# The placing of adaLN steps, three weight splits and two gate low parts in a fused attention–retention layer

## The chip, the cores and the metric

The kernel runs on one core of a Trainium2 chip as one launch. The metric is the device time of that launch in microseconds; a verdict compares medians of several runs on the same chip. One more execution was taken with the hardware profiler, and all rows shown are of that one. The engines are PE (TensorE, matrix products), DVE (VectorE), ACT (ScalarE), POOL (GpSimd) and SP (SyncE, which here issues the DMAs). Each engine works through its own list of instructions strictly in order; semaphores hold an instruction until what it needs has been written.

## The reference

The layer takes 1024 tokens of width 1024, in float32. What matters here:

```python
mod = silu(c) @ w_ada + b_ada                  # adaLN: shift1, scale1, gate1, shift2, scale2, gate2
h = rmsnorm(x, norm1_w) * (1 + scale1) + shift1
proj = h @ w_in                                # qa ka va | iq ik iw | qr kr vr gr | ga gb
qa, ka, iq, ik = partial_rope(...)             # rotation of the first 16 of 64 channels of a head
# per block of 128 tokens: index scores choose 256 keys for each token
s_h   = einsum('bqhd,bsd->bqhs', iq, ik) * idx_scale
score = einsum('bqh,bqhs->bqs', iw * w_scale, relu(s_h))
idx   = top_k(score, 256)
att   = sparse attention of qa over the chosen keys of ka, va
ret   = chunkwise retention of rotated qr, kr with vr
x = x + gate1 * ((sigmoid(ga) * (att @ w_attn_proj)
                  + sigmoid(gb) * (groupnorm(ret) * silu(gr) @ w_ret_proj)) @ w_out)
x = x + gate2 * swiglu_ffn(rmsnorm(x) * (1 + scale2) + shift2);  out = rmsnorm(x)
```

## The kernel before

Every large product is made of float32 numbers split in two parts: ACT copies a weight tile to a rounded high part (`whi`), POOL or DVE subtracts to get the low part (`wlo`), and PE forms hi·hi, hi·lo and lo·hi. `split_weight` (L77 the ACT copy, L80 the POOL subtraction) does it for tiles of 128x512, `split_block` (L958, L959) for the later streams.

A recording layer lists every instruction with a priority and writes out one fixed order per engine; `turns_after(ins, other)` only demands that `ins` stands behind `other` in the order of its engine. So an edit in one place can move instructions on several engines.

**Stage one: V and index scores.** The loop over the eight token tiles t (before L776) computes the projection to `va`, eight steps k of three products (L126, L128, L129). `behind_units` interleaves, about 11 for 8 steps, the units of the index scores. A score block b (2 to 7) begins with four PE transposes (L588), from which ACT copies two halves (`qst`, L592) and DVE subtracts the two other halves (L593). Then comes a unit for each of eight heads and one or two column chunks: two PE products into one of the PSUM buffers `lg` (L600, L601), a ReLU on ACT (L604) to one of three buffers `rl`, and a sum on DVE into `score` (L606 for the first head, L608 for the others).

In the same loop `mod_step()` takes one step of `mod_work`, the adaLN of the four vectors m = 2, 5, 3, 4 (gate1, gate2, shift2, scale2). For each m there are eight macc steps: a 128x1024 DVE instruction (L701 for the first, L703 for the rest) that multiplies `mw`, a 512 KB block of `w_ada`, into the accumulator `macc`. They are called k0 to k7 below. `mw` has two buffers: with step n SP issues the load of block n + 1 (L691), which must wait until step n − 1 has read the buffer. Each macc step is ordered behind the score sum that was recorded last. A ninth step ends the two gate vectors: `mod_gate` lets PE add `macc` over the partitions by two products with ones (L745, each 128x512) and DVE add them to the bias (L746). Before the change each tile t calls `mod_step()` twice. After each tile ACT copies the V result (L783) and SP stores it (L784).

Ahead of the loop `first_qk` loads and splits three weight slots for the retention's q and k, which are used behind the loop.

**Stage two: streams.** A stream computes 256 columns of a projection by a Strassen-like scheme: seven products M1 to M7 of 512-blocks, each of 12 matmuls (L1044 hi·hi, L1046 lo·hi of the activations, L1048 with `wlo`). `factor` makes the weight operand of a product (sums on DVE at L1002 and L1012, then `split_block`); `run` prepares three products ahead. The streams follow each other: gr (four), qa (two), ka (two), one of gb, and then ga (four, the first of them n = 9). `genv.lo_engine` says which engine makes the low part; it is None, that is POOL, for the stream n = 9. During n = 9 the rotation of q and k is also worked off: `rope_turn` twice (one per half of the tokens), each with four products on POOL (L1195 to L1198), two sums on DVE (L1200, L1201), splits (L958, L959) and stores. `passes` are DVE's counting passes of the top-256 search over `score` (L639, L644, L659), which run beside all this.

## Time and profile before

| | |
|---|---|
| three runs | 1683.88, 1686.71, 1686.22 us; median 1686.22 us |
| profiled execution | 1683.85 us, span 1682.1 us |
| granted TensorE clock | 0.999 |
| busy share of the span | PE 98%, DVE 72%, POOL 51%, ACT 45% |
| DMA | 260.70 MB, mean 155 GB/s |

A row of the timeline reads: start in us from the span's beginning, duration, engine, line, operation, the tile written and the tiles read, shapes, a count (neighbouring equal instructions are taken together), and in brackets the idle time of the engine before it with what ended it. Matmuls overlap: back to back, the next one starts while the one before is still shown as running.

### The profile page before, as it was taken

Reading aid. Unit: us, or ns where it says so; the run is one execution under the profiler, and the core shown is the slowest. Engines: PE = TensorE matmul, PEld = TensorE weight load, DVE = VectorE, ACT = ScalarE, POOL = GpSimd, SP = SyncE. Lnnn points to the kernel's source line nnn. Section 1 sums busy time; section 2 is a strip of 40 time slices with the busy share of each in tenths; the row PEclk is TensorE's granted clock in tenths of the full one; section 3 lists DMA queues with packets and bytes.
Section 4 is the critical chain, followed back from the end, with each engine's and each line's share of the span. In section 5 each row is a group of like instructions: output and inputs, shape, how many; then the busy total and the mean of one; then the engine's idle time right before and its main releaser. Section 6 shows DMA issues by size and latency. Waiting matters only on the chain.

```text
span 1682.1 us, 24430 instructions
## 1 busy us (share of the span) xinstructions
PE 1656.4 (98%) x8251; PEld 1384.8 (82%) x8251; DVE 1209.9 (72%) x2033; ACT 756.1 (45%) x1464; POOL 854.3 (51%) x842
## 2 busy tenths in 40 slices
PE   7999999999999999999999999999999999999998
PEld 6988788888888887888888888888888888888887
DVE  6549887878994879784665858966655566697675
ACT  4646533434452444420785347634333333445444
POOL 5660494974252795130355910255455455657573
PEclk9999999999999999999999999999999999999999
DMA  9554424423342555963955700245444443696652
GB/s 305 192 166 152 127 63 147 148 54 91 107 125 83 157 186 177 314 175 111 211 117 212 264 26 1 76 138 183 155 144 162 152 150 138 203 308 215 206 152 105
DMA packets 178653, 260.70 MB, mean 155 GB/s; under 512 B 13712, under 2 KB 109408, under 8 KB 176224
## 3 DMA queue, kind: packets, MB, share of 16 engines
q1 hardware_dynamic: 178272, 258.85, 49.3%
q8 instruction: 65, 1.06, 0.3%
q14 instruction: 60, 0.49, 0.1%
q10 hardware_dynamic: 256, 0.30, 0.1%
HBM read 192.51 MB, written 66.58 MB: 154 GB/s over the span
## 4 chain that ended last, share of the span: by engine, by line
PE 91%; DVE 3%; issue 2%; DMA 1%; ACT 1%; POOL 1%; SPq 0%; POOLq 0%; DVEq 0%; ACTq 0%
PE ya L1046 5%; PE mm L128 5%; PE mm L126 5%; PE ya L1044 5%; PE mm L129 5%; PE ya L1048 5%; PE yb L1044 3%; PE yb L1046 3%; PE yb L1048 3%; PE ya L1952 3%; PE ya L1953 3%; PE mm L1048 3%; PE ya L1954 2%; PE mm L1044 2%; PE mm L1046 2%; PE mm L139 2%
## 5 line engine op out<-in xcount | busy, mean ns | idle before, releaser
L80 POOL TENSOR_TENSOR wlo<-wraw,whi 128x512 fp32r<-128x512 f32 (+1 forms) x93 | 127.3, 1383 | 156.3 <-ACT whi L77 149.8
L639 DVE TENSOR_SCALAR_CACHE_REDUCE eq<-score,cand 128x384 uint8<-128x384 f32 (+2 forms) x192 | 180.8, 942 | 3.7
L959 POOL TENSOR_TENSOR flo<-tmp,fhi 128x512 fp32r<-128x512 f32 x79 | 107.8, 1365 | 140.5 <-ACT fhi L958 98.5
L126 PE MATMUL mm<-whi,hT_hi 128*128 128x512 f32 (+1 forms) x408 | 155.2, 384 | 0.0
L129 PE MATMUL mm<-whi,hT_lo 128*128 128x512 f32 (+1 forms) x408 | 153.9, 378 | 0.0
L128 PE MATMUL mm<-wlo,hT_hi 128*128 128x512 f32 (+1 forms) x408 | 153.7, 379 | 0.0
L1046 PE MATMUL ya<-hc,fhi 128*128 128x512 f32 x344 | 134.0, 389 | 0.6 <-DVE hc L1584 0.6
L1044 PE MATMUL ya<-hc,fhi 128*128 128x512 f32 x344 | 133.6, 389 | 0.3 <-DVE c L1027 0.3
L1048 PE MATMUL ya<-hc,flo 128*128 128x512 f32 x344 | 132.9, 389 | 0.0
L1928 ACT ACTIVATE dslot<-draw 128x512 fp32r<-128x512 f32 x143 | 84.6, 627 | 93.3 <-DMA draw<-act_d 31.8
L959 POOL TENSOR_TENSOR flo<-raws,fhi 128x512 fp32r<-128x512 f32 x60 | 87.1, 1458 | 72.9 <-ACT fhi L958 37.7
L1929 DVE TENSOR_TENSOR dslot<-draw,dslot 128x512 fp32r<-128x512 f32 x81 | 91.4, 1164 | 42.4 <-ACT dslot L1928 39.7
L1929 POOL TENSOR_TENSOR dslot<-draw,dslot 128x512 fp32r<-128x512 f32 x62 | 94.6, 1539 | 51.2 <-ACT dslot L1928 50.0
L958 ACT ACTIVATE fhi<-tmp 128x512 fp32r<-128x512 f32 x82 | 51.5, 629 | 111.5 <-PE ya L1046 57.2
L1044 PE MATMUL yb<-hc,fhi 128*128 128x512 f32 x256 | 99.6, 389 | 0.0
L1046 PE MATMUL yb<-hc,fhi 128*128 128x512 f32 x256 | 99.6, 389 | 0.0
L1048 PE MATMUL yb<-hc,flo 128*128 128x512 f32 x256 | 99.4, 389 | 0.0
L77 ACT ACTIVATE whi<-wraw 128x512 fp32r<-128x512 f32 (+1 forms) x94 | 55.7, 611 | 85.4 <-DMA wraw<-in_w_in_dram 29.7
L1012 DVE TENSOR_TENSOR tmp<-raws 128x512 f32<-128x512 f32 x40 | 30.6, 768 | 87.0 <-POOL flo L959 87.0
L129 PEld LDWEIGHTS mm<-whi,hT_lo 128*128 128x128 f32 x408 | 76.7, 188 | 12.0
L128 PEld LDWEIGHTS mm<-wlo,hT_hi 128*128 128x128 f32 x408 | 76.7, 188 | 11.2 <-issue 0.2
L126 PEld LDWEIGHTS mm<-whi,hT_hi 128*128 128x128 f32 x408 | 76.5, 188 | 11.2 <-PE lg L745 0.2
(474 smaller groups left out, 4875.8 us busy)
## 6 DMA issues: line engine op xcount, KB each, us to landing
draw<-act_d SPq DMA_DIRECT2D x70, 256.0 KB
mw<-in_w_ada_dram SPq DMA_DIRECT2D x32, 512.0 KB
act_d<-c SPq DMA_DIRECT2D x58, 256.0 KB
raw<-in_w_in_dram SPq DMA_DIRECT2D x26, 512.0 KB
raws<-in_w_ffn_gate_dram SPq DMA_DIRECT2D x24, 512.0 KB
raws<-in_w_ffn_up_dram SPq DMA_DIRECT2D x24, 512.0 KB
dw<-in_w_ffn_down_dram SPq DMA_DIRECT2D x22, 512.0 KB
dw_d<-dw SPq DMA_DIRECT2D x10, 1024.0 KB
```

The source lines that it names most:

```text
L77: last_split[0] = ins = nc.scalar.activation(hi[:, :n], raw[:, :n], AF.Copy)
L80: last_low[0] = low = (low_eng or nc.gpsimd).tensor_sub(lo[:, :n], raw[:, :n], f32(hi[:, :n]))
L126: ins = nc.tensor.matmul(ps, lhsT=ahi, rhs=whi[:, :n], start=(i == 0), stop=False)
L128: nc.tensor.matmul(ps, lhsT=ahi, rhs=wlo[:, :n], start=False, stop=False)
L129: nc.tensor.matmul(ps, lhsT=alo, rhs=whi[:, :n], start=False, stop=(i == last))
L639: ins = [nc.vector.tensor_scalar(eq[:, :sc.shape[1]], sc, thr[j], None, op0=op, op1=ALU.add, accum_out=cnt[:, j:j + 1]) for j, sc in enume ...
L959: return ins, (eng or nc.gpsimd).tensor_sub(lo, src, f32(hi))
L1044: mm = nc.tensor.matmul(ps, lhsT=whi[:, k, :], rhs=hhi[:, k, :], start=own and k == 0, stop=False, skip_group_check=True)
L1046: nc.tensor.matmul(ps, lhsT=whi[:, k, :], rhs=hlo[:, k, :], start=False, stop=False, skip_group_check=True)
L1048: nc.tensor.matmul(ps, lhsT=wlo[:, k, :], rhs=hhi[:, k, :], start=False, stop=k == 3, skip_group_check=True)
L1928: nc.scalar.activation(slot[:, 0], raw, AF.Copy)
L1929: ins = lo_eng.tensor_sub(slot[:, 1], raw, f32(slot[:, 0]))
```

## The change

Three things are changed. The calls of `mod_step()` per tile go from 2 each to a table, 0, 3, 3, 3, 3, 2, 1, 1, sixteen in all as before. The three ACT splits of `first_qk` are ordered behind the second, third and fourth ReLU of the scores. And in stream n = 9 the low parts of two products, those prepared right after `lo_engine` is set at M1 and at M6 (by the look-ahead of three these are M7 and M4), are made by DVE and no longer by POOL.

```diff
-    first_qk = [qk_slot(0, k) for k in range(3)]
+    first_qk, first_split = [], []
+    for k in range(3):
+        first_qk.append(qk_slot(0, k))
+        first_split.append(last_split[0])
+    MOD_AT = (0, 3, 3, 3, 3, 2, 1, 1)
...
-        for _ in range(2):
+        for _ in range(MOD_AT[t]):
             mod_step()
...
     for _ in sgen:
         pass
+    for k, ins in enumerate(first_split):
+        turns_after(ins, relus[1 + k])
...
             if m == "M1":
                 flow[n + 1].open()
                 flow[n].next = flow[n + 1]
+            if n == 9 and m in ("M1", "M5", "M6", "M3"):
+                genv.lo_engine = nc.vector if m in ("M1", "M6") else None
```

Line numbers of the changed kernel are 5 to 9 higher behind these places (L958/L959 become L965/L966, L1002 L1009, L1012 L1019, L1027 L1034, L1044/L1046/L1048 become L1051/L1053/L1055, L1200/L1201 L1207/L1208).

The order on the engines moves at three places. The first is the gate product L745 on PE, in the V loop. `mm_1701` is the V result of tile t = 3, `lg` the PSUM buffers, `macc` the accumulator of gate1. Before, no L745 stands behind that tile; it follows the next tile, 46 rows later:

```order
L600 MATMUL lg_1794<-khi_958,qst_1703 128x384
L601 MATMUL lg_1794<-klo_959,qst_1703 128x384
L126 MATMUL mm_1701<-whi_1452,hT_hi0_119 128x512
L128 MATMUL mm_1701<-wlo_1453,hT_hi0_119 128x512
L129 MATMUL mm_1701<-whi_1452,hT_lo0_120 128x512
L600 MATMUL lg_1813<-khi_958,qst_1703 128x256
```

After, on PE at the same place:

```order
L600 MATMUL lg_1794<-khi_958,qst_1703 128x384
L601 MATMUL lg_1794<-klo_959,qst_1703 128x384
L126 MATMUL mm_1701<-whi_1452,hT_hi0_119 128x512
L128 MATMUL mm_1701<-wlo_1453,hT_hi0_119 128x512
L129 MATMUL mm_1701<-whi_1452,hT_lo0_120 128x512
L745 MATMUL lg_1809<-macc_1574,spare_932 128x512
L745 MATMUL lg_1812<-macc_1574,spare_932 128x512
L600 MATMUL lg_1819<-khi_958,qst_1703 128x256
```

The two gate products now stand directly behind tile 3's last V product, with score unit `lg_1794` just ahead of that.

The second is DVE at the same time. Before, the steps k4 (`mw_1582`) and k5 (`mw_1692`) stand around the start of score block 4, k6 (`mw_1695`) and k7 (`mw_1803`) later, with score sums between them:

```order
L608 SCALAR_TENSOR_TENSOR score3_926<-rl_1686,iws_1202,score3_926 128x512
L703 SCALAR_TENSOR_TENSOR macc_1506<-mw_1582,colT_78,macc_1506 128x1024
L606 TENSOR_SCALAR score4_927<-rl_1716,iws_1202 128x384
L606 TENSOR_SCALAR score4_927<-rl_1722,iws_1202 128x256
L593 TENSOR_TENSOR qst_1853<-tr_1854,qst_1853 64x512
L613 TENSOR_TENSOR score3_926<-score3_926,cm01_931 128x128
L703 SCALAR_TENSOR_TENSOR macc_1506<-mw_1692,colT_78,macc_1506 128x1024
L608 SCALAR_TENSOR_TENSOR score4_927<-rl_1731,iws_1202,score4_927 128x384
```

```order
L608 SCALAR_TENSOR_TENSOR score4_927<-rl_1797,iws_1202,score4_927 128x384
L703 SCALAR_TENSOR_TENSOR macc_1506<-mw_1695,colT_78,macc_1506 128x1024
L608 SCALAR_TENSOR_TENSOR score4_927<-rl_1816,iws_1202,score4_927 128x256
L608 SCALAR_TENSOR_TENSOR score4_927<-rl_1822,iws_1202,score4_927 128x384
L703 SCALAR_TENSOR_TENSOR macc_1506<-mw_1803,colT_78,macc_1506 128x1024
```

After, on DVE, the steps k3 (`mw_1579`), k4 (`mw_1687`) and k5 (`mw_1692`) at the first place, then k6 (`mw_1695`), k7 (`mw_1803`) and the two L746 at the second:

```order
L593 TENSOR_TENSOR qst_1859<-tr_1860,qst_1859 64x512
L703 SCALAR_TENSOR_TENSOR macc_1574<-mw_1579,colT_78,macc_1574 128x1024
L606 TENSOR_SCALAR score4_927<-rl_1722,iws_1202 128x256
L608 SCALAR_TENSOR_TENSOR score4_927<-rl_1731,iws_1202,score4_927 128x384
L613 TENSOR_TENSOR score3_926<-score3_926,cm01_931 128x128
L703 SCALAR_TENSOR_TENSOR macc_1574<-mw_1687,colT_78,macc_1574 128x1024
L608 SCALAR_TENSOR_TENSOR score4_927<-rl_1740,iws_1202,score4_927 128x256
L608 SCALAR_TENSOR_TENSOR score4_927<-rl_1749,iws_1202,score4_927 128x384
L703 SCALAR_TENSOR_TENSOR macc_1574<-mw_1692,colT_78,macc_1574 128x1024
```

```order
L608 SCALAR_TENSOR_TENSOR score4_927<-rl_1797,iws_1202,score4_927 128x384
L703 SCALAR_TENSOR_TENSOR macc_1574<-mw_1695,colT_78,macc_1574 128x1024
L703 SCALAR_TENSOR_TENSOR macc_1574<-mw_1803,colT_78,macc_1574 128x1024
L746 TENSOR_TENSOR gateb_1690<-gateb_1690,lg_1809 128x512
L746 TENSOR_TENSOR gateb_1690<-gateb_1690,lg_1812 128x512
```

k0 and k1 have moved the other way: before they stood ahead of the first L593, after they stand behind five sums of score block 2.

The third is the stream n = 9. On DVE, `wraw_6728` (L1002, after L1009) is the sum of a factor whose split ACT makes next; `kept` are sums of products. Before:

```order
L639 TENSOR_SCALAR eq_2311,cnt_2309<-score5_928,cand_2307 128x768
L1201 TENSOR_TENSOR wlo_6490<-wlo_6490,whi_6489 128x512
L639 TENSOR_SCALAR eq_2311,cnt_2309<-score6_929,cand_2307 128x896
L1027 TENSOR_TENSOR kept_4889<-kept_4889,mm_6582 128x512
L1012 TENSOR_TENSOR wraw_6918<-raw4_4884 128x512
L639 TENSOR_SCALAR eq_2311,cnt_2309<-score7_930,cand_2307 128x1024
L1002 TENSOR_TENSOR wraw_6728<-raw4_4883,wraw_6728 128x512
L644 TENSOR_SCALAR rej_2308<-cnt_2309 128x6
```

After, on DVE:

```order
L1208 TENSOR_TENSOR wlo_6490<-wlo_6490,whi_6489 128x512
L639 TENSOR_SCALAR eq_2311,cnt_2309<-score3_926,cand_2307 128x512
L1034 TENSOR_TENSOR kept_4890<-kept_4890,lg_6610 128x512
L639 TENSOR_SCALAR eq_2311,cnt_2309<-score4_927,cand_2307 128x640
L1019 TENSOR_TENSOR wraw_6918<-raw4_4884 128x512
L639 TENSOR_SCALAR eq_2311,cnt_2309<-score5_928,cand_2307 128x768
L1009 TENSOR_TENSOR wraw_6728<-raw4_4883,wraw_6728 128x512
L639 TENSOR_SCALAR eq_2311,cnt_2309<-score6_929,cand_2307 128x896
L1034 TENSOR_TENSOR kept_4889<-kept_4889,mm_6582 128x512
L639 TENSOR_SCALAR eq_2311,cnt_2309<-score7_930,cand_2307 128x1024
```

The sum now stands ahead of two L639 and one `kept` sum that stood ahead of it, and the two new low parts stand earlier on DVE. On PE the first product with the next stream's `whi_6841` stood, before, behind M6's twelve products (`S2`):

```order
L1048 MATMUL mm_6768<-S2_5128,wlo_6731 128x512
L1044 MATMUL lg_6864<-hT_hi0_119,whi_6804 128x512
L1046 MATMUL lg_6864<-hT_lo0_120,whi_6804 128x512
L1044 MATMUL mm_6904<-hT_hi0_119,whi_6841 128x512
L1044 MATMUL lg_6790<-S4_5129,whi_6764 128x512
```

After, on PE, behind M5's (`S1`), 24 rows earlier:

```order
L1055 MATMUL lg_6790<-S1_4431,wlo_6709 128x512
L1051 MATMUL lg_6864<-hT_hi0_119,whi_6804 128x512
L1053 MATMUL lg_6864<-hT_lo0_120,whi_6804 128x512
L1051 MATMUL mm_6904<-hT_hi0_119,whi_6841 128x512
L1053 MATMUL mm_6904<-hT_lo0_120,whi_6841 128x512
```

On POOL the two subtractions `wlo_6607<-wraw_6604,whi_6606` and `wlo_6651<-wraw_6558,whi_6650` (L959) are gone from between the products of `rope_turn`, and the second `rope_turn`'s four products stand in another order.

## The prediction

> **What bounds the kernel now.** I read the page first, its engines and its chain of work that ended last:

> ```profile
> PE 1656.4 (98%) x8251; PEld 1384.8 (82%) x8251; DVE 1209.9 (72%) x2033; ACT 756.1 (45%) x1464; POOL 854.3 (51%) x842
> PE 91%; DVE 3%; issue 2%; DMA 1%; ACT 1%; POOL 1%; SPq 0%; POOLq 0%; DVEq 0%; ACTq 0%
> ```

> PE sets the time. The change removes no matmul, so it can only add or remove waits of PE. Second, the waits of PE, in us in total, times, longest:

> ```profile
> PE mm L1048 <- POOL wlo L959: 2.4, 1, 2.4
> PE lg L600 <- ACT rl L604: 2.0, 3, 1.4
> PE lg L600 <- DVE qst L593: 0.9, 2, 0.6
> PE mm L1044 <- ACT kept L1024: 0.2, 1, 0.2
> ```

> These 5.5 us are all that lies where the change works; a gain is drawn from them alone. Third, the timeline of PE in the V loop:

> ```profile
> 115.86 0.45 PE L600 MATMUL lg<-khi,qst 128*128 128x384 f32 x1 [0.56 <-DVE qst L593]
> ...
> 117.54 0.44 PE L600 MATMUL lg<-khi,qst 128*128 128x384 f32 x1 [0.36 <-DVE qst L593]
> ...
> 137.68 0.45 PE L600 MATMUL lg<-khi,qst 128*128 128x384 f32 x1 [0.20 <-ACT rl L604]
> ...
> 140.72 0.44 PE L600 MATMUL lg<-khi,qst 128*128 128x384 f32 x1 [0.35 <-ACT rl L604]
> ...
> 142.42 0.34 PE L601 MATMUL lg<-klo,qst 128*128 128x384 f32 x1
> 142.60 0.40 PE L126 MATMUL mm<-whi,hT_hi 128*128 128x512 f32 x1
> ...
> 143.29 0.28 PE L600 MATMUL lg<-khi,qst 128*128 128x256 f32 x1
> ...
> 182.53 0.50 PE L600 MATMUL lg<-khi,qst 128*128 128x512 f32 x1 [1.40 <-ACT rl L604]
> ```

> From 142.60 to 143.29 three products start, one each 0.23 us, though each is shown for 0.40. So a stall of PE costs its idle time plus 0.16: 0.72 and 0.52 for the two that end on `qst`; 0.36, 0.51 and 1.56 for the three that end on a ReLU.

> **The first stalls (MOD_AT begins with 0, splits behind ReLUs).** DVE just before them:

> ```profile
> 112.42 1.28 DVE L701 TENSOR_SCALAR macc<-mw,colT 128x1024 f32<-128x1024 f32 x1 [5.76 <-DMA mw<-in_w_ada_dram]
> 113.79 1.30 DVE L703 SCALAR_TENSOR_TENSOR macc<-mw,colT,macc 128x1024 f32<-128x1024 f32 x1
> 115.12 1.28 DVE L593 TENSOR_TENSOR qst<-tr,qst 64x512 fp32r<-64x512 f32 x2
> ```

> And ACT:

> ```profile
> 116.17 0.59 ACT L592 ACTIVATE qst<-tr 64x512 fp32r<-64x512 f32 x1
> ```

> DVE waited 5.76 us for the first `mw` with k0 and then k1 at the head of its list, and the subtractions that PE needs were queued behind them until 115.12. After, k0 and k1 stand behind five score sums. On ACT three splits stood between the copies of `qst` (0.6 us each, as the copies); they go behind ReLUs. Both causes of the two stalls go: −1.25 us. The bounds are −1.25 and 0.

> **The gate product L745.** Before, PE does not wait for it. After, it stands behind V tile 3, a place that PE passed at 143.29. What it needs is k7, and DVE reads, before:

> ```profile
> 135.54 1.28 DVE L703 SCALAR_TENSOR_TENSOR macc<-mw,colT,macc 128x1024 f32<-128x1024 f32 x1
> ...
> 138.38 1.28 DVE L703 SCALAR_TENSOR_TENSOR macc<-mw,colT,macc 128x1024 f32<-128x1024 f32 x1
> 139.57 4.37 DVE L608 SCALAR_TENSOR_TENSOR score<-rl,iws,score 128x384 f32<-128x384 f32 x9
> 143.86 1.28 DVE L703 SCALAR_TENSOR_TENSOR macc<-mw,colT,macc 128x1024 f32<-128x1024 f32 x1
> ...
> 145.98 1.28 DVE L703 SCALAR_TENSOR_TENSOR macc<-mw,colT,macc 128x1024 f32<-128x1024 f32 x1
> ```

> The four steps are k4 to k7. After, k3 takes the place of the first, k4 of the second, k5 stands behind two of the nine sums, and k6 and k7 together behind the ninth, which takes the score unit that PE issues at 142.42. At best, loads in time, k6 begins at 143.86 and k7 ends at 143.86 + 2 × 1.28 = 146.4; PE was there at 143.29 with all its stalls. So the wait is at least about 3.1 us.

> The loads make it longer. One `mw` load cannot be issued until the step two earlier has ended. The DMA share from 136 to 148 us, in 40 slices of 0.3 us; SP's row of two loads; and all loads of this line from 105 to 195 us, with their issue's duration and first and last start:

> ```profile
> DMA  0000009478875309695995300000019915746877
> ```

> ```profile
> 136.84 3.17 SPq L691 DMA_DIRECT2D mw<-in_w_ada_dram  x2
> ```

> ```profile
> L691 SPq DMA_DIRECT2D mw<-in_w_ada_dram x17: 327/328/427, 107.8 to 192.0; - x17
> ```

> Two loads are issued at 136.84 and at 139.68 (136.84 + 3.17 − 0.33); their bytes end in the 14th and the 23rd slice, at 140.2 and 142.9. A load takes 3.3 us here. The first load of all, issued at 107.8, released DVE at 112.42, after 4.6 us: the upper value.

> After: k3 ends at 136.82 and k5's load is issued; it lands at 140.2. k5 runs to 141.5, and with that k7's load goes out, landing at 144.8. Of the nine sums two ran ahead of k5; the other seven take 3.4 us (7/9 of 4.37) and end at 144.9. Then k6 to 146.2, k7 to 147.5. PE arrives at 143.29 − 1.25 = 142.04 from the first stalls; since the sums in front are up to a microsecond later, ReLUs wait for `rl` buffers and PE for ReLUs, for some 0.4. So PE is there at 142.4 and waits 5.1 us. With loads of 4.6 us, k5 ends at 142.7, k7 lands at 147.3, ends at 148.6, and the wait is 6.6 us. I take +5.1, ends 3.1 and 6.6. Queued behind L745 on PE are the rest of score block 4 and all later V products, so it is a full loss; nothing else of PE's list is free.

> **The later ReLU stalls.** Tiles 5 to 7 now take 2, 1, 1 steps in place of two each, so DVE has fewer 1.28 us steps between the sums at the end. Of the 1.56 us at 182.53 I take half, −0.8, bounded by 0 and −1.56. The stalls of 0.36 and 0.51 stay and grow by the 0.4 above: +0.4.

> **The two low parts.** POOL's list before, then PE's wait on it and two later rows of PE:

> ```profile
> 625.31 1.29 POOL L959 TENSOR_TENSOR wlo<-wraw,whi 128x512 fp32r<-128x512 f32 x1
> ...
> 636.65 1.78 POOL L959 TENSOR_TENSOR wlo<-wraw,whi 128x512 fp32r<-128x512 f32 x1
> ...
> 644.36 1.26 POOL L959 TENSOR_TENSOR wlo<-raw,whi 128x512 fp32r<-128x512 f32 x1
> ```

> ```profile
> 645.67 0.50 PE L1048 MATMUL mm<-hT_hi,wlo 128*128 128x512 f32 x1 [2.40 <-POOL wlo L959]
> ...
> 650.80 0.39 PE L1048 MATMUL mm<-hT_hi,wlo 128*128 128x512 f32 x1
> ...
> 656.24 0.39 PE L1044 MATMUL mm<-hT_hi,whi 128*128 128x512 f32 x1
> ```

> The first two go to DVE. POOL saves up to 1.29 + 1.78 = 3.1 us ahead of the low part of 644.36 on which PE waited; that wait (2.40 + 0.16) and the small one behind a `kept` copy (0.2 + 0.16) can go: −2.9.

> What is late next is DVE. PE's product with the next stream's `whi` (656.24) moves 24 rows ahead, to where PE was at 650.80. That `whi` is made by ACT right behind the split of DVE's L1002 sum:

> ```profile
> 647.34 1.13 DVE L639 TENSOR_SCALAR_CACHE_REDUCE eq<-score,cand 128x896 uint8<-128x896 f32 x1
> ...
> 648.40 0.68 DVE L1027 TENSOR_TENSOR kept<-kept,mm 128x512 f32<-128x512 f32 x1
> ...
> 650.30 1.27 DVE L639 TENSOR_SCALAR_CACHE_REDUCE eq<-score,cand 128x1024 uint8<-128x1024 f32 x1
> ...
> 651.50 1.83 DVE L1002 TENSOR_TENSOR wraw<-raw,wraw 128x512 f32<-128x512 f32 x1
> ```

> The next fence has ACT's row, the one after it all low parts that DVE makes in two of its forms (ns: least, median, most).

> ```profile
> 653.90 1.66 ACT L958 ACTIVATE whi<-raw 128x512 fp32r<-128x512 f32 x3
> ```

> ```profile
> L959 DVE TENSOR_TENSOR wlo<-wraw,whi x16: 683/690/697, 440.1 to 681.6; 128x512 fp32r<-128x512 f32 x16
> L959 DVE TENSOR_TENSOR wlo<-raw,whi x13: 678/691/1776, 431.1 to 688.7; 128x512 fp32r<-128x512 f32 x13
> ```

> The sum ended at 653.33 and the `whi` at 653.90 + 0.55 = 654.5, 1.2 later. The first three rows, 1.06 + 0.60 + 1.20 = 2.9 us from start to start, now stand behind the sum; two low parts of 0.69 stand ahead, 1.3 in all with the small overlap from start to start (DVE's rows here follow each other without idle time, so nothing hides them). So the sum ends at 653.3 − 2.9 + 1.3 = 651.7 and the `whi` is there at 652.9. PE was at this work at 650.80: 2.1 us later than before, whatever it gained at 645.67, because that gain is waited away here. If one low part takes 1.78, the largest of its kind, the loss is 3.2. If the product is not reached early, the gain of 2.9 stands. I take +2.0, ends −2.9 and +3.2; the near end is the loss, since both steps of it are list orders and durations of DVE rows.

> [...]

> **The sum.** −1.25 + 5.1 + 0.4 − 0.8 + 2.0 = +5.45 us. The profiled execution took 1683.85; that gives 1689.3. The median of the three runs lies 2.4 above it; from there it would be 1691.7. I forecast the middle, 1690.5 us, which is +0.25% on the median. About 0.2%, 3.4 us, is what a measurement of this kernel can tell from no change.

> **The rivals.**
> Faster: the gate product does not wait, since k7 comes in time. For it: before, L745 did not wait though k7 also stood among sums. Against, the product's own row:

> ```profile
> L745 PE MATMUL lg<-macc,spare x4: 592/592/592, 152.3 to 153.6; 128*128 128x512 f32 x4
> ```

> From k7's end at 147.26 (145.98 + 1.28) PE had 5 us until then, and these the new place takes away. Price: the term of 5.1 goes, and with the streams' gain of 2.9 standing the sum is −1.25 − 0.4 − 2.9 = −4.55, hence 1683.85 − 4.55 = 1679.3 on the profile and about 1680.5 on the runs. It decides for faster when the wait is below 1.1 us. Chance 0.12.

> Same: the wait is at its lower end, 3.1, and PE reaches the next `whi` without waiting or waits only as long as it gained: −1.25 + 3.1 − 0.4 + (−2.9 to +1.0) = −1.5 to +2.5, about 1685 to 1688 with the shift to the runs. Chance 0.24.

> Slower by more: DVE becomes the bound in both places, by loads of 4.6 us and low parts of 1.78: −1.25 + 6.6 + 0.4 + 3.2 = +9.0, about 1694. [...] Chance 0.12.

> The change does not do what it says: the two `qst` stalls stay, since ACT's copy at 116.17 waits for PE's transposes and not for splits. Then 1.25 is missing in the gain and the sum is +6.7, 1691.8. Chance 0.07, within slower.

> My forecast itself has 0.45. Slower is 0.45 + 0.12 + 0.07 = 0.64. The likeliest case alone, gate wait 4 to 6.6 and streams 0 to +3.2, spans 1687.5 to 1694. The range that leaves out 2 in 10 takes in the same-case: 1684.5 to 1694.5.

> **What the changed profile would show.** PE's waits get a new row of L745 on DVE's `macc`, 3 to 6.6 us near 143 to 148, with the DVE rows of k6 and k7 side by side just ahead; if its idle time is under 1 us, the main term is wrong. The two rows of L600 on DVE's `qst` are gone. The row of PE on POOL's low part is gone or under 0.7, and a wait of some 2 to 5 us on ACT's `whi` appears near 648 to 653, with L1009 ending ahead of it. If the row on POOL goes and no such wait appears, the streams gained their 2.9 us. The forecast is also wrong if DVE, while PE waits at the gate, works so far ahead that the stalls behind 150 us vanish and a part of the wait comes back: at most 1.56 by the row of 182.53.

## The result and the profile after

The changed kernel is slower: 1694.43 us median (1691.63 to 1695.90, five runs) against 1685.03 us (1683.88 to 1686.71, five runs: the three listed above and two more). The ratio is 1.0054, with a 95% interval of 1.0041 to 1.0068: some 9 us. The profiled execution took 1694.43 us, span 1692.6 us, 10.5 us more than the one shown of before. The forecast was 1690.5 us, slower by 0.25%. The direction is right, but the measured time lies only 0.07 us inside the upper end of the range, 1694.5, and a term of about 4 us was missing from the sum: that the number still falls into the range is luck.

The page of the changed kernel, engines and chain:

```profile
PE 1662.9 (98%) x8251; PEld 1387.1 (82%) x8251; DVE 1213.0 (72%) x2035; ACT 755.5 (45%) x1464; POOL 853.8 (50%) x840
PE 92%; DVE 4%; issue 1%; DMA 1%; ACT 1%; SPq 0%; POOLq 0%; POOL 0%; DVEq 0%; ACTq 0%
```

PE has the same 8251 instructions and yet is busy 6.5 us longer (1662.9 against 1656.4). So the loss is not waiting alone: some matmuls ran slower. Its waits (us in total, times, longest):

```profile
PE lg L745 <- DVE macc L703: 5.2, 1, 5.2
...
PE mm L1051 <- ACT whi L965: 2.4, 1, 2.4
PE lg L600 <- ACT rl L604: 1.8, 5, 0.8
...
PE mm L1051 <- ACT kept L1031: 0.2, 1, 0.2
```

The rows of L600 on `qst` and of PE on POOL's low part are gone, as intended. In their place stand the gate product on `macc` and a product on ACT's `whi`. PE around the gate product:

```profile
142.72 0.38 PE L600 MATMUL lg<-khi,qst 128*128 128x256 f32 x1 [0.78 <-ACT rl L604]
...
144.56 0.40 PE L129 MATMUL mm<-whi,hT_lo 128*128 128x512 f32 x1
150.17 3.75 PE L745 MATMUL lg<-macc,spare 128*128 128x512 f32 x4 [5.21 <-DVE macc L703]
152.93 1.20 PE L600 MATMUL lg<-khi,qst 128*128 128x256 f32 x1
153.93 0.42 PE L601 MATMUL lg<-klo,qst 128*128 128x256 f32 x1
...
155.31 0.39 PE L129 MATMUL mm<-whi,hT_lo 128*128 128x512 f32 x1
```

DVE and SP at the same time; the steps are k3, k4, k5, and then k6 and k7 together:

```profile
138.22 1.28 DVE L703 SCALAR_TENSOR_TENSOR macc<-mw,colT,macc 128x1024 f32<-128x1024 f32 x1
...
140.41 1.28 DVE L703 SCALAR_TENSOR_TENSOR macc<-mw,colT,macc 128x1024 f32<-128x1024 f32 x1
...
143.29 1.29 DVE L703 SCALAR_TENSOR_TENSOR macc<-mw,colT,macc 128x1024 f32<-128x1024 f32 x1 [0.67 <-DMA mw<-in_w_ada_dram]
144.50 3.01 DVE L608 SCALAR_TENSOR_TENSOR score<-rl,iws,score 128x256 f32<-128x256 f32 x6
147.42 2.60 DVE L703 SCALAR_TENSOR_TENSOR macc<-mw,colT,macc 128x1024 f32<-128x1024 f32 x2
```

```profile
139.53 5.41 SPq L691 DMA_DIRECT2D mw<-in_w_ada_dram  x3
```

k3 ends, the load for k5 goes out at 139.53 and holds DVE until 143.29; score sums follow; k6 and k7 end at 150.02, and L745 starts at 150.17. Now the windows: length, busy time of PE, PEld, DVE, ACT, POOL (instructions), and then the granted clock of PE, the DMA share and GB/s:

```profile
140.00:145.00 5.00, 3.89 (x19) 2.72 (x17) 4.33 (x8) 1.61 (x4) 0.00 (x0) 1.00 0.70 201
145.00:150.00 5.00, 0.00 (x0) 0.00 (x0) 4.90 (x7) 1.75 (x4) 0.00 (x0) 0.81 0.60 179
150.00:151.00 1.00, 0.83 (x1) 0.50 (x2) 0.02 (x1) 0.00 (x0) 0.00 (x0) 0.50 0.64 201
...
153.00:154.00 1.00, 1.00 (x4) 0.48 (x3) 0.04 (x1) 0.00 (x0) 0.00 (x0) 0.50 0.31 123
154.00:155.00 1.00, 1.00 (x5) 1.00 (x5) 0.84 (x2) 0.38 (x1) 0.00 (x0) 0.55 0.00 0
155.00:156.00 1.00, 1.00 (x6) 0.83 (x6) 0.74 (x2) 0.52 (x2) 0.00 (x0) 1.00 0.53 217
```

While PE stands idle, from 144.96 to 150.17, its granted clock falls to 0.50, and it stays there until 154.9, for 4.7 us after PE resumes. The four records of L745 take 3.75 us from the first start to the last end; before, the same four took 1.88 us (592 ns for each, overlapping). In the stream n = 9 the same happens on a smaller scale:

```profile
656.85 0.39 PE L1053 MATMUL lg<-hT_lo,whi 128*128 128x512 f32 x1
659.64 0.50 PE L1051 MATMUL mm<-hT_hi,whi 128*128 128x512 f32 x1 [2.40 <-ACT whi L965]
...
664.32 0.39 PE L1055 MATMUL mm<-hT_hi,wlo 128*128 128x512 f32 x1
```

```profile
659.60:661.00 1.40, 1.36 (x4) 1.14 (x5) 1.40 (x2) 0.51 (x1) 1.40 (x2) 0.67 0.65 233
661.00:663.00 2.00, 2.00 (x6) 1.52 (x6) 2.00 (x4) 1.03 (x2) 2.00 (x2) 0.50 0.53 203
```

DVE's sum and ACT's split that PE waits for:

```profile
657.52 0.83 DVE L1009 TENSOR_TENSOR wraw<-raw,wraw 128x512 f32<-128x512 f32 x1
```

```profile
658.44 0.63 ACT L965 ACTIVATE whi<-wraw 128x512 fp32r<-128x512 f32 x1 [1.94 <-DVE wraw L1009]
658.98 1.14 ACT L965 ACTIVATE whi<-raw 128x512 fp32r<-128x512 f32 x2
```

### The profile page after: what moved, and what is told of

It is laid out like the page before. It is cut to its first block, busy times and chain, and to the rows that moved or that the text cites. A ratio compares the mean times of both kernels' runs of the same rounds, so it can differ in the third digit from the quotient of the medians.

```text
span 1692.6 us, 24422 instructions
## 1 busy us (share of the span) xinstructions
PE 1662.9 (98%) x8251; PEld 1387.1 (82%) x8251; DVE 1213.0 (72%) x2035; ACT 755.5 (45%) x1464; POOL 853.8 (50%) x840
## 3 DMA queue, kind: packets, MB, share of 16 engines
q8 instruction: 65, 1.06, 0.3%
## 4 chain that ended last, share of the span: by engine, by line
PE 92%; DVE 4%; issue 1%; DMA 1%; ACT 1%; SPq 0%; POOLq 0%; POOL 0%; DVEq 0%; ACTq 0%
PE mm L126 5%; PE mm L128 5%; PE mm L129 5%; PE ya L1053 5%; PE ya L1055 4%; PE ya L1051 4%; PE yb L1055 3%; PE yb L1051 3%; PE yb L1053 3%; PE mm L1051 3%; PE ya L1961 3%; PE mm L1053 2%; PE mm L1055 2%; PE ya L1963 2%; PE ya L1962 2%; PE mm L139 2%
## 5 line engine op out<-in xcount | busy, mean ns | idle before, releaser
L639 DVE TENSOR_SCALAR_CACHE_REDUCE eq<-score,cand 128x384 uint8<-128x384 f32 (+2 forms) x192 | 180.7, 941 | 3.5
L966 POOL TENSOR_TENSOR flo<-tmp,fhi 128x512 fp32r<-128x512 f32 x79 | 108.0, 1367 | 142.1 <-ACT fhi L965 100.1
L126 PE MATMUL mm<-whi,hT_hi 128*128 128x512 f32 (+1 forms) x408 | 155.2, 384 | 0.0
L1053 PE MATMUL ya<-hc,fhi 128*128 128x512 f32 x344 | 133.9, 389 | 0.6 <-DVE hc L1593 0.6
L1051 PE MATMUL ya<-hc,fhi 128*128 128x512 f32 x344 | 133.6, 389 | 0.3 <-DVE c L1034 0.3
L1055 PE MATMUL ya<-hc,flo 128*128 128x512 f32 x344 | 132.9, 389 | 0.0
L966 POOL TENSOR_TENSOR flo<-raws,fhi 128x512 fp32r<-128x512 f32 x60 | 86.9, 1454 | 71.4 <-ACT fhi L965 37.5
L965 ACT ACTIVATE fhi<-tmp 128x512 fp32r<-128x512 f32 x82 | 51.5, 629 | 111.5 <-PE ya L1053 58.0
L1051 PE MATMUL yb<-hc,fhi 128*128 128x512 f32 x256 | 99.6, 389 | 0.0
L1053 PE MATMUL yb<-hc,fhi 128*128 128x512 f32 x256 | 99.6, 389 | 0.0
L1055 PE MATMUL yb<-hc,flo 128*128 128x512 f32 x256 | 99.4, 389 | 0.0
L1019 DVE TENSOR_TENSOR tmp<-raws 128x512 f32<-128x512 f32 x40 | 30.6, 768 | 85.9 <-POOL flo L966 85.9
L126 PEld LDWEIGHTS mm<-whi,hT_hi 128*128 128x128 f32 x408 | 76.7, 188 | 11.2 <-PE lg L745 0.2
```

Of the source, the lines that this page charges most:

```text
L126: ins = nc.tensor.matmul(ps, lhsT=ahi, rhs=whi[:, :n], start=(i == 0), stop=False)
L639: ins = [nc.vector.tensor_scalar(eq[:, :sc.shape[1]], sc, thr[j], None, op0=op, op1=ALU.add, accum_out=cnt[:, j:j + 1]) for j, sc in enume ...
L966: return ins, (eng or nc.gpsimd).tensor_sub(lo, src, f32(hi))
L1051: mm = nc.tensor.matmul(ps, lhsT=whi[:, k, :], rhs=hhi[:, k, :], start=own and k == 0, stop=False, skip_group_check=True)
L1053: nc.tensor.matmul(ps, lhsT=whi[:, k, :], rhs=hlo[:, k, :], start=False, stop=False, skip_group_check=True)
L1055: nc.tensor.matmul(ps, lhsT=wlo[:, k, :], rhs=hhi[:, k, :], start=False, stop=k == 3, skip_group_check=True)
```

## The experiments

Each was timed against the kernel before in several rounds on one chip. The ratios are given with their 95% intervals; differences in us are between medians.

**Steps alone.** The changed kernel without the splits' order and without the low parts:

```diff
-    for k, ins in enumerate(first_split):
-        turns_after(ins, relus[1 + k])
...
-            if n == 9 and m in ("M1", "M5", "M6", "M3"):
-                genv.lo_engine = nc.vector if m in ("M1", "M6") else None
```

> The changed kernel without the ordering of the three splits and without the two low parts on VectorE: only the table of adaLN steps. Theory A (the loss is the gate product's wait plus the half clock behind it): PE waits about 5 us at L745 and runs at half clock for some 4 us behind it; +5 to +8 us against the kernel before. Rival B (the loss sits in the stream n = 9, the V loop is even): -1.5 to +1 us. Rival C (the parts need each other): anything, but then steps, splits and lows alone do not add up to about +9.

Measured: 1691.56 against 1684.29 us, ratio 1.0046 (1.0033 to 1.0059), +7.3 us. Its waits and windows:

```profile
PE lg L745 <- DVE macc L703: 5.1, 1, 5.1
...
PE mm L1053 <- POOL wlo L964: 1.4, 1, 1.4
...
PE lg L600 <- DVE qst L593: 0.7, 1, 0.7
...
PE tr L588 <- DVE qst L593: 0.5, 1, 0.5
```

```profile
143.00:149.00 6.00, 1.11 (x6) 0.63 (x4) 5.90 (x9) 1.75 (x4) 0.00 (x0) 0.75 0.62 198
149.00:153.00 4.00, 3.81 (x6) 1.77 (x7) 0.75 (x3) 0.00 (x0) 0.00 (x0) 0.52 0.71 252
```

The step table alone brings the wait, the half clock and most of the loss: theory A. One stall of L600 on `qst` stays, and the transposes of a score block (L588) wait for `qst` too, for 0.5 us. The changed kernel, which edits this stage further by the splits' order alone, has neither row.

**Splits alone.** Steps two per tile, no low parts on DVE; only the order of the splits is kept.

```diff
-    MOD_AT = (0, 3, 3, 3, 3, 2, 1, 1)
+    MOD_AT = (2, 2, 2, 2, 2, 2, 2, 2)
...
-            if n == 9 and m in ("M1", "M5", "M6", "M3"):
-                genv.lo_engine = nc.vector if m in ("M1", "M6") else None
```

> Only the ordering of the three splits behind ReLUs; steps two per tile and the low parts as before. Theory A: DVE's k0 and k1 still stand ahead of the first qst subtraction, so the first of the two qst stalls stays; -0.6 to 0 us. Rival B (the copies on ACT were the cause of both stalls): -1.25 us and no row of L600 on qst. Both are below what a timing can tell, so the wait rows decide.

Measured: 1685.00 against 1684.29 us, ratio 1.0006 (0.9997 to 1.0015), no difference. The rows decide: here too one `qst` stall stays, now behind k0 and k1 at the head of DVE's list. So each of the two edits alone leaves a stall, and only both together remove both, which is theory A's mechanism; rival B is out. The median, +0.7 us, lies above theory A's range of -0.6 to 0, but its interval, -0.5 to +2.5 us, overlaps it.

```profile
115.81 0.44 PE L600 MATMUL lg<-khi,qst 128*128 128x384 f32 x1 [0.58 <-DVE qst L593]
```

This profile also held something that no theory spoke of. Its wait on POOL's low part was shorter than before, 1.8 us, and yet the clock fell behind it:

```profile
PE mm L1055 <- POOL wlo L966: 1.8, 1, 1.8
```

```profile
646.00:650.00 4.00, 4.00 (x12) 3.17 (x11) 4.00 (x8) 2.83 (x6) 4.00 (x4) 0.59 0.76 223
```

**Low parts alone.** Steps two per tile, splits as before; only the two low parts are on DVE.

```diff
-    MOD_AT = (0, 3, 3, 3, 3, 2, 1, 1)
+    MOD_AT = (2, 2, 2, 2, 2, 2, 2, 2)
...
-    for k, ins in enumerate(first_split):
-        turns_after(ins, relus[1 + k])
```

> Only the two low parts of the stream n = 9 on VectorE. Theory A: the wait of 2.4 us on POOL's low part is gone and one of 2 to 3 us on ACT's whi behind the VectorE sum takes its place, with half clock behind it where the gate falls shut; 0 to +3 us. Rival B: the wait of 2.9 us is won: -2.9 us.

Measured: 1686.40 against 1684.29 us, ratio 1.0013 (1.0004 to 1.0023), +2.1 us. The wait on POOL is replaced by one on `whi`, with half clock behind it in this profile:

```profile
PE mm L1049 <- ACT whi L963: 2.4, 1, 2.4
```

```profile
652.50:656.00 3.50, 3.48 (x8) 2.80 (x9) 3.50 (x5) 2.26 (x5) 3.50 (x3) 0.51 0.55 208
```

The three parts alone add up to 7.3 + 0.7 + 2.1 = 10.1 us, against 9.4 measured for all together: no sign that the loss needs them together (rival C of the first experiment).

**The gate product one tile later.** All as changed, but the eighth step and the ninth, which carries the gate product, fall a tile later:

```diff
-    MOD_AT = (0, 3, 3, 3, 3, 2, 1, 1)
+    MOD_AT = (0, 3, 3, 2, 4, 2, 1, 1)
```

> The changed kernel with one number moved: steps per tile 0, 3, 3, 2, 4, 2, 1, 1, so that the ninth step with the gate product stands behind V tile 4 and not behind tile 3; all else as changed. Theory A: the wait at L745 goes (k7 is long done) and the half clock with it; 7 to 8 us faster than the changed kernel, so -0.5 to +3 us against the kernel before. Rival B (VectorE as a whole is late and PE waits for it somewhere else): the wait turns up at the ReLUs, and the time stays at +6 to +9 us.

Measured: 1684.87 against 1684.29 us, ratio 1.0007 (0.9999 to 1.0016). The loss is gone but for what cannot be told from nothing. The waits have no row of L745:

```profile
PE mm L1051 <- ACT whi L965: 2.4, 1, 2.4
PE lg L600 <- ACT rl L604: 2.1, 5, 0.8
```

The mean granted clock is 0.999, against 0.996 in the changed kernel. Three and even four steps in a tile cost nothing that can be told here; the place of PE's product did. Theory A.

**Filling the wait.** The changed kernel with twenty products more, in front of the gate product:

```diff
             gp = ps_lg()
+            if i == 0 and hf == 0:
+                for _ in range(20):
+                    nc.tensor.matmul(gp, lhsT=hT.lhs(3)(0)[0], rhs=slots[0][0][:, :H], start=True, stop=True)
             nc.tensor.matmul(gp, lhsT=ones, rhs=acc[:, cs], start=True, stop=True)
```

> The changed kernel with twenty products more: right ahead of the gate product, PE multiplies a finished activation tile with a finished weight tile into the gate's own PSUM buffer (0.23 us each, 4.6 us in all), and the gate product then overwrites it. Nothing of the result uses them. Theory A (PE's idle stretch of 5.2 us throws the clock to one half, and that costs 2.2 us behind it): L745 starts when it did, the idle stretch before it is 0.6 us or less, the clock behind it stays at 1.00; 2.2 us faster than the changed kernel, +5.5 to +8 us against the kernel before. Rival B (the slow products behind L745 come from the gate product's own form or from its neighbours): they stay slow, and the time stays at +8 to +10 us or grows by the added work.

Measured: 1690.49 against 1684.07 us, ratio 1.0036 (1.0023 to 1.0048): +6.4 us, where the changed kernel without these products has +9.4. The two intervals overlap a little, so the rows carry the proof: more work on the engine that bounds the kernel, and less time lost. PE and the clock:

```profile
144.58 4.87 PE L747 MATMUL lg<-whi,hT_hi 128*128 128x512 f32 x20 [0.65 <-ACT rl L604]
149.28 1.88 PE L748 MATMUL lg<-macc,spare 128*128 128x512 f32 x4
...
152.04 0.40 PE L129 MATMUL mm<-whi,hT_lo 128*128 128x512 f32 x1
```

```profile
145.00:150.00 5.00, 5.00 (x22) 3.86 (x21) 3.89 (x5) 0.82 (x2) 0.00 (x0) 1.00 0.59 198
150.00:152.00 2.00, 2.00 (x9) 1.34 (x8) 1.49 (x3) 0.56 (x2) 0.00 (x0) 1.00 0.86 322
```

From the start of the gate product to the same V product behind it: 152.04 − 149.28 = 2.76 us here, 155.31 − 150.17 = 5.14 us in the changed kernel. The half clock at this place costs 2.4 us. In this profile the clock stayed at full also behind the wait for `whi`; from that wait's end to the fourteenth product it took 659.80 − 656.67 = 3.13 us, and in the changed kernel 664.32 − 659.64 = 4.68 us, so the fall there cost 1.55 us. The filler products stand 500 us ahead of that place; why the clock did not fall there, the views of this profile do not show.

```profile
656.67 0.50 PE L1054 MATMUL mm<-hT_hi,whi 128*128 128x512 f32 x1 [2.41 <-ACT whi L968]
...
659.80 0.39 PE L1058 MATMUL mm<-hT_hi,wlo 128*128 128x512 f32 x1
```

**Steps moved, low parts left on POOL.** An attempt at a version better than both:

```diff
-    MOD_AT = (0, 3, 3, 3, 3, 2, 1, 1)
+    MOD_AT = (0, 2, 3, 3, 3, 2, 2, 1)
...
-            if n == 9 and m in ("M1", "M5", "M6", "M3"):
-                genv.lo_engine = nc.vector if m in ("M1", "M6") else None
```

> The changed kernel with the steps per tile 0, 2, 3, 3, 3, 2, 2, 1 (the gate product behind V tile 4) and without the two low parts on VectorE; the splits' order as changed. Theory A (with the gate product one tile later only the gain of the first stalls is left, and the low parts had cost): the two qst stalls of 1.25 us are gone, no wait at L745, the stream n = 9 waits on POOL as before; -2.5 to 0 us against the kernel before. Rival B (a step taken out of the first tile always comes back as a wait at ReLUs): 0 to +2 us.

Measured: 1683.29 against 1684.07 us, ratio 0.9997 (0.9988 to 1.0006): no difference that can be told. The `qst` stalls are gone, and the ReLU waits have grown from 2.0 to 3.1 us:

```profile
PE lg L600 <- ACT rl L604: 3.1, 5, 1.4
...
PE mm L1055 <- POOL wlo L966: 1.8, 1, 1.8
```

So both expectations hold in part: the stalls' 1.25 us are won, and 1.1 us more are waited at the ReLUs. No version that beats the kernel before was found.

## Why the prediction was right, and where its sizes were off

The sum was +5.45 us; the profiles differ by 10.5 and the medians by 9.4. Its terms, one by one (a stall of PE counted as its idle time plus 0.16, as in the prediction):

- *First stalls, −1.25.* Right: no row of L600 on `qst` is left, −1.24. The two experiments with one edit each show that it takes both the step table and the splits' order.
- *Gate product, +5.1.* Right in place, cause and size: 5.21 + 0.16 = 5.4. One step was inexact and did no harm: k7's load was forecast to end just when the sums did; in the trace k6 and k7 run back to back, so at the end the sums decide, and of the loads only k5's held DVE, for 0.67 us. Both ends of the wait came some 2.5 us later than forecast, PE's arrival at 144.96 and not at 142.4, k7's end at 150.02 and not at 147.5; that they shifted alike was not foreseen. A slip in the bounds: the 6.6 us leaves out the 0.4 us of ReLU waits that the 5.1 takes in; with them it is 6.2. The experiment with the product a tile later shows the cause.
- *Half clock.* This term is missing from the sum, and it is the step that failed: I priced a wait at its length. Behind the gate product it is 2.4 us, shown by filling the wait, and 1.55 us behind the wait of 2.40 us for `whi`, together 4.0 of the 10.5 us between the two profiles; behind waits of that length it followed in some profiles and not in others (last section). At the gate product the trace shows 5.2 us of idle time, and 0.50 from 148.07 to 154.89.
- *ReLU stalls ahead of the gate, +0.4.* Too small: of the five waits of 1.8 us in all, four lie ahead of the gate and make 1.6, with 0.16 for each 2.2, against 0.9 before: +1.4.
- *The later ReLU stall, −0.8.* Nearer to its bound: the 1.56 us at 182.53 are gone, and the fifth wait, 0.2 + 0.16, stands instead: −1.2.
- *Stream n = 9, +2.0.* The replaced wait came as described, but its working was too dear: it implied a wait of 5.0 us (the loss of 2.1 and the gain of 2.9), and 2.40 was measured. DVE's sum took 0.83 us where the row of before had 1.83, which makes 1.0 of these 2.6 us; the rest was not put down to rows. So the stream came out about even by waits, 2.6 + 0.3 against 2.9, and lost 1.55 by the clock. The low parts alone cost 2.1 us in the timed runs. That is the forecast number, reached by another way. The two low parts took 0.68 and 0.73 us on DVE; all eighteen of their form there took 681 to 730 ns.

These terms make −1.2 + 5.4 + 2.4 + 1.4 − 1.2 + 0 + 1.55 = +8.3. Of the other 2.2 us between the two profiles, 0.93 lie ahead of the V loop, where the change moves nothing: the same product (L126) starts at 107.39 before and at 108.32 after. At the start of the kernel products of 512 columns begin 0.42 us apart, as they do at half clock in the changed kernel from 660.32 to 662.88, until 19.8 us in the profile of before and until 21.8 in that of after, when each trace records its first change of the clock (the views print 1.00 ahead of that); this is the single execution and not the change. The remaining 1.3 us were not put down to rows, and the runs of the changed kernel alone spread over 4.3 us.

Of the rivals, "faster" needed a wait under 1.1 us at the gate and falls with 5.2; "same" needed 3.1. The rival "slower by more", +9.0, has the right size for the wrong reason, loads of 4.6 us and low parts of 1.78. k5's load took 3.8 us (139.53 to 143.29), and neither of the two low parts took 1.78. The rival that the `qst` stalls stay falls with their rows.

## What to carry to other kernels

Where every engine has one fixed order, moving a step earlier moves its consumers earlier too; ask of each consumer on the bounding engine what still has to be done for its operand when the engine reaches the new place. Price an idle stretch of PE as its length plus what the clock behind it costs: here half clock took 2.4 us behind a wait of 5.21 us, and 1.55 us behind one of 2.40 us, where it followed; twenty filler products in the gap brought 3.0 us between the medians. When a producer is taken off one engine, look at the other inputs of the same stretch first: POOL's 2.4 us wait became ACT's 2.4 us wait behind DVE.

## What the runs showed of the hardware

The clock fell behind short waits too, and not always. Waits of 2.4 us were followed by half clock in the changed kernel (0.50 over 661 to 663) and in the kernel with the low parts alone (0.51 over 652.5 to 656), and not in the kernel before (1.00 over 644.48 to 651.31), in the one with the gate late (1.00 over 648 to 653), and in the one with the filled wait (products 0.23 us apart from 657.01 to 659.80); a wait of 1.8 us on the same low part was followed by it in one kernel (splits alone, 0.59 over 646 to 650) and not in another (steps moved, 1.00 over 643 to 650).

```profile
641.07:644.48 3.41, 2.21 (x10) 1.50 (x8) 3.34 (x7) 0.63 (x1) 3.41 (x4) 1.00 0.44 151
644.48:647.89 3.41, 2.22 (x10) 1.84 (x11) 3.41 (x7) 1.01 (x2) 3.41 (x3) 1.00 0.65 217
647.89:651.31 3.42, 3.42 (x17) 2.84 (x16) 3.42 (x5) 2.82 (x6) 3.42 (x3) 1.00 0.72 210
```

```profile
656.65:660.07 3.42, 1.02 (x5) 0.47 (x4) 3.42 (x8) 1.63 (x3) 3.42 (x3) 1.00 0.81 211
660.07:663.48 3.41, 3.41 (x10) 2.73 (x9) 3.41 (x4) 1.56 (x4) 3.41 (x3) 0.50 0.51 196
```

The window's length less PE's busy time (the first two numbers behind the window) is PE's idle time in it. It is 1.20 and 1.19 us before, and no half clock follows; it is 2.40 in the changed kernel, and half clock follows. Over these two traces, from the first change of the clock on, it stood at half behind every window with 2.10 us of idle time or more (3.11 and 2.10 at the gate product, the 2.40 shown, and 3.32 and 3.41 in the last full window of the kernel before and of the changed kernel) and behind none with 1.49 or less; no window lies between, and the ends of matmuls are modelled. Where a grid lay in the other six profiles, their views do not show. An estimate from these numbers: a wait of 1.8 or 2.4 us costs half clock by the luck of where a boundary falls, while one of 5.2 us, cut in the middle, would still leave 2.6 us in a window, more than the 2.10 behind which half clock was seen. In the window from 656.65 us, with half clock behind it, PE was busy for 1.02 of 3.42 us.
